# Decoder layer on one core: order of the negated pieces of u and of their adding transfers in the up projection

## The chip, the cores and the metric

The kernel runs on one core of one Trainium2 chip. The metric is the device time of one launch in microseconds (us), the median of several runs. Below, PE is TensorE (matmuls; PEld its weight loads), DVE is VectorE, ACT is ScalarE, POOL is GpSimd and SP is SyncE. SP, ACT and POOL each issue DMA transfers from their own instruction streams; a transfer that has to wait holds everything that stands behind it in that stream.

## The reference, cut to what matters

One decoder layer for 256 tokens of width 2048. Attention, the first residual and its norms come first; the change lies in the MLP behind them, with `d_ff` = 8192:

```
h = _rmsnorm(x, norm_mlp_pre[layer])
u = jnp.square(jax.nn.relu(h @ w_up[layer]))
x = x + _rmsnorm(u @ w_down[layer], norm_mlp_post[layer])
```

All data are float32. The kernel computes each product of float32 matrices from two rounded parts of each operand, hi = round(a) and lo = a - hi, as three matmuls: hi*hi, hi*lo, lo*hi.

## The kernel before

**Up projection.** The loop over `j` takes eight chunks of 1024 columns of `w_up`. A chunk accumulates four outputs of 128 tokens x 512 columns in PSUM (`acc_u`, for two token blocks b and two column halves n). Some 128-row blocks of the weights are multiplied directly ("k" steps, 12 matmuls each). Pairs of others go through a scheme with seven products instead of eight (`seven_products`, the "w" steps), for which DVE first builds sums of the weight blocks (`t` and `u` tiles, L361, L365, L366), and some of the products go to four more banks `m`. At a chunk's end `close` (L1052, L1055) combines the `m` banks into a tile `c`, and four DVE additions (L1121) put them into `acc_u`.

**Weights.** A "k" step's weights are loaded by SP into one of five `raw` buffers (512 KB). A "w" step's weights are loaded by POOL into one of two buffers, `ab` and `ab2` (1 MB, L374), or, in the last two chunks, partly by SP. ACT writes the hi part (L306, or L310 with a gain), and DVE the lo part (L307, L311). There are eight hi and eight lo buffers.

**Hand-over between chunks.** `up_evac` takes each `acc_u` of the finished chunk while PE already works on the next chunk: ACT writes r = relu(acc_u * scale) (L937) into one of two buffers `r`, PE transposes r (`rt`, L300), and ACT squares the transposes into the tile `uT` (L949; for some blocks the tile is called `u`, `ab` or `ab2`). The two halves n of chunk j give the blocks g = 2j and g = 2j+1 of u, each 128 x 1024.

**The low parts of u.** The down projection needs hi and lo of u. For every block g but the first, `lo_away(g)` prepares lo ahead of time in DRAM (`ukeep`): for each half h of the block, ACT writes -round(u) into an `r` buffer (`neg`, L960), ACT issues the write of it to `ukeep` (256 KB, L962), and POOL issues a transfer that adds u itself to the same place of `ukeep` (L964), so that u - round(u) stands there. POOL must wait for the write to land before it issues the add. Much later `split_u` brings the result back with one transfer per block (`ulo`, L976). `ukeep` transfers share POOL's stream with the loads of `ab` and `ab2`, and `neg` shares the two `r` buffers with `up_evac`.

**What sets the order.** There is no scheduler on the chip: each engine executes its instructions in the order in which the program wrote them. `Flow` sets that order while the program is built. The matmuls advance a planned clock (`flow.spend`); side work is written as generators whose `yield` gives the planned delay until their next piece; `pump` writes the pieces that have come due between two groups of matmuls. So a number in a `yield`, or the delay given to `flow.start`, decides behind which instructions a piece stands in its engine's stream, not when it runs.

Of the kernel before, what the change touches and what calls it, by code (L numbers as in the profile page):

```python
# [263 lines left out]
def layer(nc, tc, io):  # L264
    flow = Flow()
# [12 lines left out]
    def bank(i, name):  # L278
        return ps.tile([P, 512], F32, tag=f"bank{i}", bufs=1, name=name)
# [19 lines left out]
    def transpose(out, a):  # L299
        nc.tensor.transpose(out, a, ident)  # L300
        flow.spend(TR)
# [631 lines left out]
    def up_evac(j, b, i, acc, order):  # L933

        yield UP_STEP * order
        r = late["up"].tile([P, 512], F32, tag="r", bufs=2, name=f"r{j}_{b}")
        nc.scalar.activation(r, acc, AF.Relu, scale=rstd2[b])  # L937
        yield D_UP if j > 1 else 2 * D_UP
        t = bank(i, f"rt{j}_{b}")
        for k in range(4):  # L940
            transpose(t[:, k * P:(k + 1) * P], r[:, k * P:(k + 1) * P])
        if j not in uT:
            if j in (0, 1, 10, 11, 12, 13):
                t2 = late["u01" if j < 2 else "ab2" if j < 12 else "ab"][:, j % 2 * CW:(j % 2 + 1) * CW]
            else:
                tag = {"tag": "T", "bufs": 2} if j > 13 else {}
                t2 = late["up"].tile([P, CW], F32, name=f"uT{j}", **tag)
            uT[j] = t2.rearrange("p (k s) -> p k s", k=4)
        nc.scalar.activation(uT[j][:, :, b * P:(b + 1) * P], t.rearrange("p (k s) -> p k s", k=4), AF.Square)  # L949
        if b and j:  # L950
            flow.start(lo_away(j), 5.0 + 7.0 * (j % 2))

    def lo_away(g):

        ukeep[g] = dram.tile([P, CW], F32, name=f"ukeep{g}")
        u = uT[g].rearrange("p k s -> p (k s)")
        for h in range(2):
            c = slice(h * 512, (h + 1) * 512)
            t = late["up"].tile([P, 512], F32, tag="r", bufs=2, name=f"neg{g}_{h}")
            nc.scalar.activation(t.bitcast(F32R), u[:, c], AF.Copy, scale=-1.0)  # L960
            yield 1.0
            nc.scalar.dma_start(out=ukeep[g][:, c], in_=t)  # L962
            yield 9.0
            nc.gpsimd.dma_start(out=ukeep[g][:, c], in_=u[:, c], accum_op=OP.add)  # L964
            yield 2.0

# [96 lines left out]
    for j in range(FF // CW):  # L1063
# [9 lines left out]
        for t, b in order:  # L1073
# [19 lines left out]
            if what == "k":  # L1093
                w = weights.get(tiles[0])
                h_done(k, b)
                for n in range(2):
                    c = slice(n * 512, (n + 1) * 512)
                    three(accs[b, n], [tok(hT[x], k, b) for x in range(2)], [w[x][:, 0, c] for x in range(2)], t == 0, t == len(steps) - 1)
                    if j == 0 and t == len(steps) - 1:
                        evac.append(flow.start(up_evac(n, b, at[b, n], accs[b, n], 2 * b + n - 0.25 * (2 * b + n))))  # L1100
                    flow.pump()
                if b == NB - 1:
                    weights.free(tiles[0])
                continue
# [13 lines left out]
        if j:  # L1118

            for bn in PARTS:  # L1120
                nc.vector.tensor_tensor(out=accs[bn], in0=accs[bn], in1=more[bn], op=OP.add)  # L1121
            for o, (b, n) in enumerate(PARTS):
                evac.append(flow.start(up_evac(2 * j + n, b, at[b, n], accs[b, n], o + 0.6)))
# [194 lines left out]
```

## Time and profile before

| | |
|---|---|
| median of 3 runs | 1054.12 us (1051.59 to 1059.64) |
| profiled execution: its own time | 1057.15 us |
| profiled execution: span of the trace | 1055.2 us |
| granted TensorE clock, mean | 0.997 |
| busy in the span | PE 1035.3, DVE 834.4, ACT 645.3, POOL 90.0 us |
| up projection in the trace | roughly 365 to 715 us |
| down projection in the trace | roughly 715 to 1040 us |

Times in the trace count from the start of the span. A timeline row gives the start, the duration, the engine, the line and operation with output and input, how often, and in brackets the idle time of that engine just before and what ended it. A row of the chain of waits gives start, duration and what the end of the program was waiting for in that stretch.

### The profile page before, as it was taken

The numbers are of one execution on the slowest core, as the hardware profiler recorded it, in microseconds if no ns is written. First come the engines' busy times: TensorE is split into PE (matmuls) and PEld (weight loads), VectorE is DVE, ScalarE is ACT, GpSimd is POOL, SyncE is SP. The second block draws the span as 40 slices with busy tenths as digits, with TensorE's granted clock in tenths as the row PEclk, the third lists the DMA queues.
The fourth block names the chain that finished last, engine by engine and source line by source line (L and its number), as shares of the span: only waits on it lengthen the run. The fifth ranks groups of instructions, "written<-read, shape, count | busy, mean of one in ns | idle before, by whom it ended". The sixth has DMA issues, their size and how long they took to land.

```text
span 1055.2 us, 13457 instructions
## 1 busy us (share of the span) xinstructions
PE 1035.3 (98%) x4828; PEld 859.5 (81%) x4828; DVE 834.4 (79%) x1122; ACT 645.3 (61%) x884; POOL 90.0 (9%) x134
## 2 busy tenths in 40 slices
PE   9999999999999999999999999899999999999996
PEld 6888899888888788888877778787888888888885
DVE  6776546577556679998989889788889888998895
ACT  6675436566454567576756667667666664867661
POOL 0000000000000000111110111011110101111100
PEclk9999999999999999999999999999999999999998
DMA  9974546454356295758778687589997977789872
GB/s 303 369 232 147 147 131 222 145 175 152 129 197 221 86 374 160 242 169 287 221 235 251 201 249 196 189 273 353 305 333 271 358 251 244 287 302 344 339 240 80
DMA packets 89395, 248.21 MB, mean 235 GB/s; under 512 B 7920, under 2 KB 12528, under 8 KB 88944
## 3 DMA queue, kind: packets, MB, share of 16 engines
q1 hardware_dynamic: 61984, 162.03, 45.3%
q0 software_dynamic: 22592, 77.08, 23.4%
q10 hardware_dynamic: 4752, 8.24, 2.1%
q8 instruction: 38, 0.62, 0.2%
q14 instruction: 29, 0.24, 0.1%
HBM read 222.16 MB, written 25.17 MB: 234 GB/s over the span
## 4 chain that ended last, share of the span: by engine, by line
PE 78%; DVE 10%; DMA 6%; issue 3%; ACT 2%; POOL 0%; ACTq 0%; DVEq 0%; SPq 0%; POOLq 0%
PE y L296 24%; PE acc_u L296 11%; PE acc_o L296 8%; PE md L296 6%; PE acc_qk L296 4%; PE acc_v L296 4%; DVE lo L307 3%; PE m L296 3%; PE acc_ckv L296 2%; DVE lo L311 2%; DMA raw<-in_w_up 2%; PE acc_ukv L296 2%; PE acc_q L296 2%; PE acc_cq L296 2%; PE acc_k L296 2%
## 5 line engine op out<-in xcount | busy, mean ns | idle before, releaser
L307 DVE TENSOR_TENSOR lo<-raw,hi 128x1024 fp32r<-128x1024 f32 (+3 forms) x207 | 233.8, 1150 | 81.8 <-ACT hi L306 80.7
L306 ACT ACTIVATE hi<-raw 128x1024 fp32r<-128x1024 f32 (+3 forms) x207 | 203.4, 997 | 69.3 <-DMA raw<-in_w_in 14.4
L296 PE MATMUL acc_u<-hi,hT_hi 128*128 128x512 f32 x356 | 142.0, 399 | 0.4 <-DVE c L1055 0.4
L296 PE MATMUL acc_u<-hi,hT_lo 128*128 128x512 f32 x356 | 139.2, 391 | 0.4 <-DVE hT_lo L307 0.4
L296 PE MATMUL acc_u<-lo,hT_hi 128*128 128x512 f32 x356 | 138.8, 390 | 0.0
L296 PE MATMUL y<-hi,uhi 128*128 128x512 f32 x352 | 137.3, 390 | 0.0
L296 PE MATMUL y<-hi,ulo 128*128 128x512 f32 x352 | 137.0, 389 | 0.0
L296 PE MATMUL y<-lo,uhi 128*128 128x512 f32 x352 | 136.9, 389 | 0.0
L311 DVE SCALAR_TENSOR_TENSOR lo<-raw,gcol,hi 128x1024 fp32r<-128x1024 f32 x74 | 92.6, 1279 | 12.7 <-ACT hi L310 12.7
L310 ACT ACTIVATE hi<-raw,gcol 128x1024 fp32r<-128x1024 f32 x74 | 82.9, 1145 | 27.8 <-DMA raw<-in_w_up 21.1
L296 PEld LDWEIGHTS acc_u<-hi,hT_lo 128*128 128x128 f32 x356 | 66.8, 188 | 15.2 <-DVE hT_lo L307 0.8
L296 PEld LDWEIGHTS acc_u<-hi,hT_hi 128*128 128x128 f32 x356 | 66.9, 188 | 14.1 <-DVE c L1055 1.4
L296 PEld LDWEIGHTS acc_u<-lo,hT_hi 128*128 128x128 f32 x356 | 67.0, 188 | 12.7
L296 PEld LDWEIGHTS y<-lo,uhi 128*128 128x128 f32 x352 | 66.1, 188 | 13.7
L296 PEld LDWEIGHTS y<-hi,ulo 128*128 128x128 f32 x352 | 66.1, 188 | 13.7
L296 PEld LDWEIGHTS y<-hi,uhi 128*128 128x128 f32 x352 | 66.1, 188 | 13.6
L306 ACT ACTIVATE hi<-u 128x1024 fp32r<-128x1024 f32 (+1 forms) x38 | 37.6, 991 | 61.1 <-DVE u L366 47.4
L307 DVE TENSOR_TENSOR lo<-st_down,hi 128x1024 fp32r<-128x1024 f32 x48 | 57.6, 1220 | 1.5 <-ACT hi L306 1.5
L306 ACT ACTIVATE hi<-st_down 128x1024 fp32r<-128x1024 f32 x48 | 50.0, 1050 | 3.5 <-DVE st_down L366 1.1
L296 PE MATMUL md<-hi,s 128*128 128x512 f32 x144 | 52.1, 389 | 0.0
L296 PE MATMUL acc_o<-hi,mixT_hi 128*128 128x512 f32 x128 | 51.8, 405 | 0.0
L296 PE MATMUL acc_o<-hi,mixT_lo 128*128 128x512 f32 x128 | 50.2, 392 | 0.0
(330 smaller groups left out, 2167.9 us busy)
## 6 DMA issues: line engine op xcount, KB each, us to landing
raw<-in_w_down SPq DMA_DIRECT2D x80, 512.0 KB, 6.4
raw<-in_w_up SPq DMA_DIRECT2D x76, 512.0 KB, 5.8
raw<-in_w_in SPq DMA_DIRECT2D x55, 512.0 KB, 4.9
ab<-in_w_up POOLq DMA_DIRECT2D x22, 1024.0 KB, 8.0
raw<-in_w_out SPq DMA_DIRECT2D x32, 512.0 KB, 4.4
ulo<-ukeep POOLq DMA_DIRECT2D x30, 512.0 KB, 6.2
ab_down<-in_w_down POOLq DMA_DIRECT2D x13, 1024.0 KB, 9.4
ukeep<-neg ACTq DMA_DIRECT2D x30, 256.0 KB, 5.5
```

Source lines behind the costliest of these rows:

```text
L296: nc.tensor.matmul(out, a, b, start=start, stop=stop)
L306: nc.scalar.activation(hi, src, AF.Copy)
L307: nc.vector.tensor_tensor(out=lo, in0=src, in1=hi.bitcast(F32), op=OP.subtract)
L310: nc.scalar.activation(hi, src, AF.Copy, scale=g)
L311: nc.vector.scalar_tensor_tensor(out=lo, in0=src, scalar=g, in1=hi.bitcast(F32), op0=OP.mult, op1=OP.subtract)
```

## The change

In `up_evac`, `lo_away(j)` starts 2.0 planned us (even blocks) or 6.0 (odd blocks) after a block is complete, instead of 5.0 or 12.0. In `lo_away`, both halves are now negated and written first, with 8.0 planned us from one half to the next instead of 12.0, and only after a further 16.0 planned us are the two adding transfers issued, 2.0 apart.

```
@@ -948,7 +948,7 @@
         if b and j:
-            flow.start(lo_away(j), 5.0 + 7.0 * (j % 2))
+            flow.start(lo_away(j), 2.0 + 4.0 * (j % 2))
@@ -960,7 +960,10 @@
             nc.scalar.activation(t.bitcast(F32R), u[:, c], AF.Copy, scale=-1.0)
             yield 1.0
             nc.scalar.dma_start(out=ukeep[g][:, c], in_=t)
-            yield 9.0
+            yield 7.0
+        yield 16.0
+        for h in range(2):
+            c = slice(h * 512, (h + 1) * 512)
             nc.gpsimd.dma_start(out=ukeep[g][:, c], in_=u[:, c], accum_op=OP.add)
             yield 2.0
```

No instruction is added or removed. The streams of PE, DVE and SP keep their order; only ACT's and POOL's change. Behind the change, line numbers from L964 on are three higher. Three places follow.

POOL in chunk 3, from the load of its fourth pair of weight blocks (`ab2_3503`) to the load of chunk 4's third pair (`ab_3502`). `ukeep4` and `ukeep5` are the blocks that chunk 2 produced. Before:

```order
L374 DMA ab2_3503<-in_w_up 128x2x1024
L964 DMA ukeep4_4589<-uT4_4485 128x512
L964 DMA ukeep5_4672<-uT5_4505 128x512
L374 DMA ab_3502<-in_w_up 128x2x1024
L964 DMA ukeep4_4589<-uT4_4485 128x512
L964 DMA ukeep5_4672<-uT5_4505 128x512
L374 DMA ab2_3503<-in_w_up 128x2x1024
L374 DMA ab_3502<-in_w_up 128x2x1024
```

After:

```order
L374 DMA ab2_3503<-in_w_up 128x2x1024
L374 DMA ab_3502<-in_w_up 128x2x1024
L967 DMA ukeep4_4553<-uT4_4483 128x512 x2
L374 DMA ab2_3503<-in_w_up 128x2x1024
L967 DMA ukeep5_4621<-uT5_4503 128x512 x2
L374 DMA ab_3502<-in_w_up 128x2x1024
```

The load of chunk 4's first pair (`ab`, the second load shown) no longer has an add ahead of it, and the load of its second pair (`ab2`, the third load shown) stands behind the two adds of block 4 instead of behind all four.

ACT in chunk 3, from the last square of block 5 on. `hi192` to `hi195` are the hi parts of chunk 3's second pair, `hi197` and `hi198` those of its third. Before:

```order
L949 ACTIVATE uT5_4505<-rt5_1_4545 128x4x128
L306 ACTIVATE hi192_4558<-ab2_3503 128x512
L306 ACTIVATE hi193_4562<-ab2_3503 128x1024
L306 ACTIVATE hi194_4569<-u3_1_4520 128x1024
L306 ACTIVATE hi195_4579<-t3_1_4519 128x1024
L960 ACTIVATE neg4_0_4590<-uT4_4485 128x512
L310 ACTIVATE hi196_4600<-raw196_4598,gcol_69 128x1024
L962 DMA ukeep4_4589<-neg4_0_4590 128x512
L306 ACTIVATE hi197_4611<-ab_3502 128x512
```

After:

```order
L949 ACTIVATE uT5_4503<-rt5_1_4544 128x4x128
L960 ACTIVATE neg4_0_4554<-uT4_4483 128x512
L306 ACTIVATE hi192_4560<-ab2_3503 128x512
L306 ACTIVATE hi193_4564<-ab2_3503 128x1024
L306 ACTIVATE hi194_4572<-u3_1_4518 128x1024
L962 DMA ukeep4_4553<-neg4_0_4554 128x512
L306 ACTIVATE hi195_4583<-t3_1_4517 128x1024
L310 ACTIVATE hi196_4601<-raw196_4599,gcol_69 128x1024
L306 ACTIVATE hi197_4611<-ab_3502 128x512
L960 ACTIVATE neg5_0_4622<-uT5_4503 128x512
L962 DMA ukeep5_4621<-neg5_0_4622 128x512
```

The first half of block 4 is negated ahead of the second pair's hi parts instead of behind them, and its write is issued two rows earlier; the first half of block 5 moves forward from behind the third pair. The four halves of a chunk now end about where the third of them stood before. In chunk 7 the first `neg12` stands in the same way ahead of `uhi0`, the hi part of u's block 0.

ACT at the end of chunk 7, where `c_3504<-m1_7` opens the combination of the `m` banks (L1052 before, L1055 after). Before:

```order
L306 ACTIVATE hi302_6297<-raw302_6295 128x1024
L306 ACTIVATE hi303_6310<-raw303_6308 128x1024
L1052 ACTIVATE c_3504<-m1_7_6120 128x512
L306 ACTIVATE hi304_6327<-raw304_6325 128x1024
L960 ACTIVATE neg13_1_6334<-ab_3502 128x512
L962 DMA ukeep13_6212<-neg13_1_6334 128x512
L306 ACTIVATE hi305_6349<-raw305_6347 128x1024
```

After:

```order
L306 ACTIVATE hi302_6299<-raw302_6297 128x1024
L306 ACTIVATE hi303_6311<-raw303_6309 128x1024
L1055 ACTIVATE c_3504<-m1_7_6124 128x512
L306 ACTIVATE hi304_6328<-raw304_6326 128x1024
L306 ACTIVATE hi305_6346<-raw305_6344 128x1024
L306 ACTIVATE hi306_6380<-raw306_6378 128x1024
```

The last `neg` of the chunk and its write are gone from here; they stand eight rows ahead of `c<-m`. In chunks 2 to 6 the last `neg` stood directly ahead of `c<-m`, and has moved up likewise.

More of the change, by code (lines that the diff above doesn't have):

```diff
@@ L950, in up_evac @@
         if b and j:
-            flow.start(lo_away(j), 5.0 + 7.0 * (j % 2))
+            flow.start(lo_away(j), 2.0 + 4.0 * (j % 2))
     def lo_away(g):
@@ L962, in lo_away @@
             nc.scalar.dma_start(out=ukeep[g][:, c], in_=t)
-            yield 9.0
+            yield 7.0
+        yield 16.0
+        for h in range(2):
+            c = slice(h * 512, (h + 1) * 512)
             nc.gpsimd.dma_start(out=ukeep[g][:, c], in_=u[:, c], accum_op=OP.add)
```

## The prediction

> **What bounds the kernel now.** The page's first part comes first, because it says how much is to be had at all.
>
> ```profile
> PE 1035.3 (98%) x4828; PEld 859.5 (81%) x4828; DVE 834.4 (79%) x1122; ACT 645.3 (61%) x884; POOL 90.0 (9%) x134
> ```
>
> PE is busy for 1035.3 of 1055.2 us. The change leaves PE's work alone, so it can only touch the 19.9 us in which PE idles. PE's timeline, read next for its idle times, shows where the up projection has them:
>
> ```profile
> 538.48 0.66 PE L300 MATMUL rt<-ident,r 128*128 128x128 f32 x4 [1.25 <-ACT r L937]
> 576.72 0.51 PE L296 MATMUL acc_u<-hi,hT_hi 128*128 128x512 f32 x1 [0.43 <-DVE c L1055]
> 584.02 0.66 PE L300 MATMUL rt<-ident,r 128*128 128x128 f32 x4 [1.77 <-ACT r L937]
> 628.93 0.66 PE L300 MATMUL rt<-ident,r 128*128 128x128 f32 x4 [1.76 <-ACT r L937]
> 670.77 0.66 PE L300 MATMUL rt<-ident,r 128*128 128x128 f32 x4 [1.41 <-ACT r L937]
> 677.43 0.66 PE L300 MATMUL rt<-ident,r 128*128 128x128 f32 x4 [1.40 <-ACT r L937]
> 720.08 0.66 PE L300 MATMUL rt<-ident,r 128*128 128x128 f32 x4 [1.57 <-ACT r L937]
> ```
>
> All are hand-overs: chunks 3 to 4 (1.25), 4 to 5 (0.43 + 1.77), 5 to 6 (1.76), 6 to 7 (1.41 + 1.40), 7 to the down projection (1.57). Together 9.59 us, the most that this change can win there. Each waits for r, which waits for DVE's last additions into acc_u: DVE comes late to the chunk's end. Why, the chain of waits tells:
>
> ```profile
> 482.55 6.92 DMA ukeep<-neg
> ...
> 489.99 0.54 POOL ukeep L964
> 490.53 8.26 DMA ab<-in_w_up
> 498.88 1.24 DVE t L361
> ```
>
> The write of a negated piece takes 6.92 us; POOL stands before its add all that time; the load of the chunk's second pair stands behind the add, and DVE waits for the load. One chunk later the engines' timelines show the same:
>
> ```profile
> 534.67 0.87 POOL L964 DMA_DIRECT2D ukeep<-uT  x1 [7.47 <-DMA ukeep<-neg]
> 535.21 1.07 POOL L374 DMA_DIRECT2D ab<-in_w_up  x1
> 543.70 1.23 DVE L361 TENSOR_TENSOR t<-ab 128x1024 f32<-128x1024 f32 x1 [2.58 <-DMA ab<-in_w_up]
> ```
>
> **Part 1, the late loads.** In the new order the second pair's load stands behind the two adds of the even block only. The buffer it fills was last read in the second and third of these splits, and free at 518.26 + 1.82 = 520.1; the even block's second piece now stands right behind the first of them:
>
> ```profile
> 509.45 1.06 ACT L306 ACTIVATE hi<-u 128x1024 fp32r<-128x1024 f32 x1 [2.75 <-DVE u L366]
> 513.45 1.04 ACT L306 ACTIVATE hi<-ab 128x1024 fp32r<-128x1024 f32 x1
> 518.26 1.82 DVE L307 TENSOR_TENSOR lo<-ab,hi 128x512 fp32r<-128x512 f32 x2
> ```
>
> Its write so leaves ACT near 511 to 512, and with the 6.92 us above it has landed before the buffer is free. The load starts near 520 instead of 535.21 and lands 15 us earlier. DVE's wait at the chunk's front goes. What is late next is ACT: its hi parts of that pair follow the fourth square `uT<-rt`, which PE's transposes release. How far DVE is behind that square is seen in chunks 2 (no late load) to 6, square first, then DVE's split of u:
>
> ```profile
> 456.63 0.60 ACT L949 ACTIVATE uT<-rt 128x512 f32<-128x512 f32 x1 [1.03 <-PE rt L300]
> 459.87 1.22 DVE L307 TENSOR_TENSOR lo<-u,hi 128x1024 fp32r<-128x1024 f32 x1
> 499.33 0.60 ACT L949 ACTIVATE uT<-rt 128x512 f32<-128x512 f32 x1 [0.83 <-PE rt L300]
> 504.41 1.22 DVE L307 TENSOR_TENSOR lo<-u,hi 128x1024 fp32r<-128x1024 f32 x1
> 543.53 0.60 ACT L949 ACTIVATE uT<-rt 128x512 f32<-128x512 f32 x1 [0.50 <-PE rt L300]
> 549.23 1.22 DVE L307 TENSOR_TENSOR lo<-u,hi 128x1024 fp32r<-128x1024 f32 x1
> 589.07 0.60 ACT L949 ACTIVATE uT<-rt 128x512 f32<-128x512 f32 x1 [0.50 <-PE rt L300]
> 594.86 1.22 DVE L307 TENSOR_TENSOR lo<-u,hi 128x1024 fp32r<-128x1024 f32 x1
> 633.99 0.60 ACT L949 ACTIVATE ab<-rt 128x512 f32<-128x512 f32 x1 [0.51 <-PE rt L300]
> 639.36 1.22 DVE L307 TENSOR_TENSOR lo<-u,hi 128x1024 fp32r<-128x1024 f32 x1
> ```
>
> The distance is 3.24 us in chunk 2, and 5.08, 5.70, 5.79 and 5.37 in chunks 3 to 6: DVE could be 1.84, 2.46, 2.55 and 2.13 us earlier. But the first negated piece now stands between the square and the hi parts, and costs its duration there:
>
> ```profile
> L960 ACT ACTIVATE neg<-uT x20: 612/615/618, 460.5 to 751.3; 128x512 fp32r<-128x512 f32 x20
> ```
>
> With 0.6 off, DVE gains 1.2, 1.9, 1.9 and 1.5 us. Left of the stalls: 3 to 4, 1.25 - 1.2 = 0.05; 4 to 5, 2.20 - 1.9 = 0.3; 5 to 6 none; 6 to 7 the first (1.41) none, while the second comes 1.41 us sooner on PE and its r 1.5 us sooner, so 1.40 + 1.41 - 1.5 = 1.3.
>
> **Part 2, the end of chunk 7.** No `ab` load is late there. At its front the moved piece pushes the first of these rows back by 0.6, and at its end the second row goes, which is 0.6 again on the chain to r:
>
> ```profile
> 680.44 1.05 ACT L306 ACTIVATE uhi<-u 128x1024 fp32r<-128x1024 f32 x1
> 709.91 0.62 ACT L960 ACTIVATE neg<-ab 128x512 fp32r<-128x512 f32 x1
> ```
>
> I set it even, between 1.0 (only the end counts) and 2.2 (only the front): 1.57 stays. So 0.05 + 0.3 + 0 + 1.3 + 1.57 = 3.2 us remain, and the gain would be 9.6 - 3.2 = **6.4 us**, if nothing else moved.
>
> **Part 3, the crowd at the chunk's end.** The second pair's load (1 MB) and the adds now run at about 517 to 528 of chunk 3's time, where SP fetches the last `raw` blocks that DVE splits before the additions. These leave almost no slack:
>
> ```profile
> 517.06 1.28 DVE L311 SCALAR_TENSOR_TENSOR lo<-raw,gcol,hi 128x1024 fp32r<-128x1024 f32 x1
> 522.27 6.07 DVE L311 SCALAR_TENSOR_TENSOR lo<-raw,gcol,hi 128x1024 fp32r<-128x1024 f32 x5
> 524.92 1.15 ACT L310 ACTIVATE hi<-raw,gcol 128x1024 fp32r<-128x1024 f32 x1 [0.99 <-DMA raw<-in_w_up]
> 563.18 7.79 DMA raw<-in_w_up
> 572.26 1.28 DVE L311 SCALAR_TENSOR_TENSOR lo<-raw,gcol,hi 128x1024 fp32r<-128x1024 f32 x1 [0.31 <-ACT hi L310]
> 668.10 1.28 DVE L311 SCALAR_TENSOR_TENSOR lo<-raw,gcol,hi 128x1024 fp32r<-128x1024 f32 x1 [2.21 <-ACT hi L310]
> ```
>
> The first row frees the buffer for the last fetch of chunk 3, at 518.3, and ACT uses it at 524.92: 6.6 us. In chunk 3 ACT ends the last of the five at 526.07, and DVE takes it about 1.0 later, the slack. In chunk 4 the fetch took 7.79 and DVE waited 0.31; in chunk 6 it waited 2.21. If the fetch takes x us longer, chunks 4 and 6 pay x, chunks 3 and 5 pay x - 1.0 (chunk 5, which shows no such wait, taken as chunk 3). The price was not measured in the new order. The nearest row is the landing of `raw` between 500 and 700 us, min, median, max; the second is over the whole run:
>
> ```profile
> DMA to landing us min/median/max: 3.4/6.2/9.2
> DMA to landing us min/median/max: 2.7/5.1/13.3
> ```
>
> From 7.79, x lies between -1.2 (the 6.6 us of chunk 3's fetch) and +1.4 (the 9.2). In the other direction the first pair's load leaves this stretch, by 5 us, so the bytes nearly balance; what is added are adds. I take x = +1.0, nearer the upper end because DVE is then waiting on the last of several. That costs 1.0 + 1.0 = 2.0 us, which leaves **4.4 us** of gain. The ends give 2.9 (x = 1.4) and 7.9 (x = -1.2).
>
> The Trainium skill (DMA: Bandwidth & Descriptors, section Queues, rings and completion order) says that a DMA engine serves the queues that have work in turn, packet by packet. By that, more transfers behind each other in POOL's queue would not slow SP's. By it the sum is 6.4. The two fetches above, of 6.6 and 7.8 us, each ran beside one 1 MB load and do not decide it.
>
> **Costed at nothing.** The odd block's second piece waits, as before, for an `r` buffer, that is for its first write to land:
>
> ```profile
> DMA to landing us min/median/max: 2.0/5.5/8.3
> ```
>
> By the order the two stand some 7 us apart (an estimate); at 8.3 ACT is held for 1.3 us. Behind it stands the hi of `ab` that ran at 513.45, which DVE wants near 519.1: 4 us of cover, and beyond that each us is paid on DVE. The adds that now come later are wanted only by the `ulo` transfers of the down projection, and the writes have landed before POOL reaches them.
>
> **Rivals.** *No crowd*: x = 0, 1054.12 - 6.4 = **1047.7**; for it, the moved first load frees the stretch; against it, the waits of 0.31 and 2.21 are already those of full traffic. *All stalls go*, 9.6: **1044.5**; for it, DVE's work in a chunk is less than PE's once nothing is late; against it, the hand-overs after chunks 6 and 7 have fetches and an ACT queue of their own. *The wait only changes place*: at x = 2 the rests are 1.05, 2.3, 0.9, 3.3 and 1.57, 9.1 together, the gain 0.5, **1053.6**; for it, 2.21 us of DVE's wait in chunk 6 are of this kind; against it, 9.8 us is more than any fetch here took. The same result comes if the adds still block the load, should the even writes land 9 us late. *Slower*: the same fetch at the run's longest, 13.3 (x = 5.5); chunks 3 to 6 then pay 20 us more, less the 6.4: about 13.5 lost, **1067.6**. It turns at x = 2.1, a fetch of 9.9 us; against it, 13.3 came once, and not here.
>
> **How the numbers follow.** The sums are against the profiled execution's own 1057.15 us, which makes 1052.8; it lies 3.0 above the median of the runs, 1054.12, and from that I predict 1054.12 - 4.4 = **1049.7**. Chances: forecast 0.48, no crowd 0.17, all stalls go 0.12, wait changes place 0.18, slower 0.05. The range takes in all but the last, with about 1 to 3 us for the spread of runs (1051.59 to 1059.64 before): **1043.5 to 1056.5**. A measurement of this kernel tells about 1% from no change, 10.5 us. More than that cannot come from 9.6 us, only from all of them with luck in the runs: 0.06. Slower by over 1%: 0.05. Within: 0.89.
>
> **What will show it.** Right: POOL starts a chunk's second `ab` load some 15 us earlier; no DVE wait for `ab` at the fronts of chunks 3 to 6; the distance from square to split of u near 3.8; PE's stall after chunk 3 gone and those after 4 and 5 below 1.3. DVE waits on the last `raw` fetch of chunks 4 and 6 grow by about 1 us. Wrong: the stalls stay while the wait moves to `raw` (crowd under-costed), or vanish also after chunks 6 and 7 (crowd over-costed), or ACT's hi parts wait on `neg`.

## The result and the profile after

The changed kernel takes **1050.07 us**, the median of 14 runs (1048.38 to 1051.71); 14 runs of the kernel before give 1057.32 us (1051.59 to 1061.42). The ratio is **0.9934, with a 95% interval of 0.992 to 0.9948**: 7.0 us less (5.5 to 8.5). The profiled execution took 1049.74 us, against 1057.15 before: 7.41 less. Two later sessions gave 0.9939 (0.9921 to 0.9956) and 0.9933 (0.9915 to 0.9952).

First the totals of the page. PE's work is the same; the span around it is 1047.9 us instead of 1055.2.

```profile
PE 1035.3 (99%) x4828; PEld 860.3 (82%) x4828; DVE 834.0 (80%) x1122; ACT 644.5 (62%) x884; POOL 90.4 (9%) x134
```

Then PE's timeline, all rows with idle time from 480 us on. Of seven stalls before (9.59 us) one is left. Two waits are new, in the down projection.

```profile
669.53 0.66 PE L300 MATMUL rt<-ident,r 128*128 128x128 f32 x4 [0.65 <-ACT r L937]
894.04 0.50 PE L296 MATMUL y<-lo,uhi 128*128 128x512 f32 x1 [0.74 <-DVE lo L307]
976.98 0.50 PE L296 MATMUL y<-hi,ulo 128*128 128x512 f32 x1 [0.80 <-DMA ulo<-ukeep]
```

8.94 us went and 1.54 came: 7.40, next to the 7.41 between the two executions. That holds for this one profile. In the two later profiles of the changed kernel the stall after chunk 6 is 1.38 and 1.30, the one from chunk 7 to the down projection is not gone but 0.72 and 0.27 (1.57 before), and the two waits in the down projection are absent once and 0.25 and 0.75 the other time. The cause is seen on POOL, in chunk 3: the load of the second pair starts at 519.60, not 535.21, and waits only for its buffer (DVE's lo), not for a write.

```profile
519.60 0.74 POOL L374 DMA_DIRECT2D ab<-in_w_up  x1 [3.39 <-DVE lo L307]
520.33 0.91 POOL L967 DMA_DIRECT2D ukeep<-uT  x1
524.35 0.85 POOL L967 DMA_DIRECT2D ukeep<-uT  x1 [3.12 <-DMA ukeep<-neg]
```

At the front of chunk 4 DVE then finds the load there. What it waits for is ACT, in two places of 0.28 and 0.26 us; between ACT's square and the hi parts stands the moved `neg`. (The second wait comes with only the adds moved too, 0.25 there; the first, of 0.28, does not.)

```profile
542.74 0.60 ACT L949 ACTIVATE uT<-rt 128x512 f32<-128x512 f32 x1 [0.49 <-PE rt L300]
543.23 0.63 ACT L960 ACTIVATE neg<-uT 128x512 fp32r<-128x512 f32 x1
544.40 0.69 DVE L307 TENSOR_TENSOR lo<-ab,hi 128x512 fp32r<-128x512 f32 x1 [0.28 <-ACT hi L306]
545.35 1.23 DVE L307 TENSOR_TENSOR lo<-ab,hi 128x1024 fp32r<-128x1024 f32 x1 [0.26 <-ACT hi L306]
546.50 1.22 DVE L307 TENSOR_TENSOR lo<-u,hi 128x1024 fp32r<-128x1024 f32 x1
```

The ends of the chunks: the five splits of `raw` in chunks 3 and 4 run without a gap, and in chunk 6 the wait is 1.45 (2.21 before). In chunk 6 ACT waits 4.70 for the last `raw` fetch (5.71 before), in chunk 7 4.84 (6.53 before). DVE waits 7.89 for `ab_down` at 719 (3.62 before), and PE loses nothing to it.

```profile
521.49 6.06 DVE L311 SCALAR_TENSOR_TENSOR lo<-raw,gcol,hi 128x1024 fp32r<-128x1024 f32 x5
564.35 6.06 DVE L311 SCALAR_TENSOR_TENSOR lo<-raw,gcol,hi 128x1024 fp32r<-128x1024 f32 x5
659.02 1.16 ACT L310 ACTIVATE hi<-raw,gcol 128x1024 fp32r<-128x1024 f32 x1 [4.70 <-DMA raw<-in_w_up]
660.21 1.28 DVE L311 SCALAR_TENSOR_TENSOR lo<-raw,gcol,hi 128x1024 fp32r<-128x1024 f32 x1 [1.45 <-ACT hi L310]
685.38 1.15 ACT L310 ACTIVATE hi<-raw,gcol 128x1024 fp32r<-128x1024 f32 x1 [4.84 <-DMA raw<-in_w_up]
719.04 1.22 DVE L361 TENSOR_TENSOR st_down<-ab_down 128x1024 f32<-128x1024 f32 x1 [7.89 <-DMA ab_down<-in_w_down]
```

### The profile page after: what moved, and what is told of

The parts are those of the page before. It is cut to its first block, busy times and chain, and to the rows that moved or that the text cites. A ratio compares the mean times of both kernels' runs of the same rounds, so it can differ in the third digit from the quotient of the medians.

```text
span 1047.9 us, 13455 instructions
## 1 busy us (share of the span) xinstructions
PE 1035.3 (99%) x4828; PEld 860.3 (82%) x4828; DVE 834.0 (80%) x1122; ACT 644.5 (62%) x884; POOL 90.4 (9%) x134
## 4 chain that ended last, share of the span: by engine, by line
PE 86%; DVE 6%; DMA 3%; issue 2%; ACT 2%; SPq 0%; POOL 0%; DVEq 0%; POOLq 0%; ACTq 0%
PE acc_u L296 21%; PE y L296 20%; PE acc_o L296 8%; PE m L296 6%; PE md L296 5%; PE acc_v L296 4%; PE acc_qk L296 4%; DVE lo L307 3%; PE acc_ckv L296 2%; PE acc_ukv L296 2%; PE acc_q L296 2%; PE acc_cq L296 2%; PE acc_k L296 2%; PE acc_uq L296 2%; PE rt L300 1%
## 5 line engine op out<-in xcount | busy, mean ns | idle before, releaser
L311 DVE SCALAR_TENSOR_TENSOR lo<-raw,gcol,hi 128x1024 fp32r<-128x1024 f32 x74 | 92.4, 1278 | 11.1 <-ACT hi L310 11.0
```

Of the source, the lines that this page charges most:

```text
L311: nc.vector.scalar_tensor_tensor(out=lo, in0=src, scalar=g, in1=hi.bitcast(F32), op0=OP.mult, op1=OP.subtract)
```

## The experiments

The theory is the held load: DVE is late because one load stands on POOL behind adds that wait for writes. The rivals: ACT's order alone makes the gain, or the number of transfers in one place does. The runs were made in three sessions, each on one chip beside the kernel before, which took 1058.22, 1056.63 and 1056.58 us there; so times of different sessions can be set side by side only to within some 1.6 us.

| run | median, us | ratio to before (95%) |
|---|---|---|
| only the adds moved, first session | 1047.71 | 0.990 (0.987 to 0.9929) |
| only the negated pieces moved | 1051.80 | 0.9942 (0.9919 to 0.9965) |
| before, no adds | 1046.95 | 0.9897 (0.9867 to 0.9927) |
| after, no adds | 1049.36 | 0.9913 (0.988 to 0.9946) |
| changed kernel, second session | 1049.84 | 0.9939 (0.9921 to 0.9956) |
| one add ahead of the load | 1053.74 | 0.9963 (0.9949 to 0.9977) |
| chunk 7's adds early | 1050.95 | 0.9945 (0.9926 to 0.9964) |
| delays 5.0 and 9.0 | 1048.72 | 0.9926 (0.9908 to 0.9944) |
| only the adds moved, third session | 1047.81 | 0.9908 (0.9891 to 0.9925) |
| delays 5.0 and 9.0, third session | 1048.40 | 0.9913 (0.9895 to 0.9931) |
| changed kernel, third session | 1050.82 | 0.9933 (0.9915 to 0.9952) |
| doubled crowd | 1052.57 | 0.9956 (0.9935 to 0.9976) |

### Each half of the change alone

Only the adds moved: against the kernel before, the pieces keep their places and the adds take those of the changed kernel.

```
             nc.scalar.dma_start(out=ukeep[g][:, c], in_=t)
-            yield 9.0
+            yield 11.0
+        yield 5.0 - 3.0 * (g % 2)
+        for h in range(2):
+            c = slice(h * 512, (h + 1) * 512)
             nc.gpsimd.dma_start(out=ukeep[g][:, c], in_=u[:, c], accum_op=OP.add)
```

> The negated pieces and their writes stand on ACT where they stood before; only the adds stand later on POOL, where the change puts them. Held load (my theory: DVE is late because the second ab2 load of a chunk stands on POOL behind adds that wait for the writes of negated pieces): the load now stands behind the two adds of the even block alone, whose second write leaves ACT at 518.9 in chunk 3 and lands 5 to 8 us later, so the load starts at 524 to 527 instead of 535.2. Before, DVE waited 2.58 us for it, so every start ahead of 532.6 ends that wait: 6 to 8 us less than the kernel before, as with the whole change. ACT's order (rival: the gain comes from the last negated piece, which no longer stands ahead of c<-m at the chunk's end): that piece still stands there, so no gain, 0 to 1 us.

Only the pieces moved: against the changed kernel, the adds go back to the planned times of before.

```
-            yield 7.0
-        yield 16.0
+            yield 7.0 * (1 - h)
+        yield 4.0 + 3.0 * (g % 2)
         for h in range(2):
             c = slice(h * 512, (h + 1) * 512)
             nc.gpsimd.dma_start(out=ukeep[g][:, c], in_=u[:, c], accum_op=OP.add)
-            yield 2.0
+            yield 12.0
```

> The negated pieces and their writes stand on ACT where the change puts them; the adds keep the planned times of before, so that the ab2 load stands behind all four of them again. Held load: the last of the four writes leaves ACT at 516.5 of chunk 3 instead of 526.6 and lands 4 to 9 us later, so the load starts at 521 to 526, still ahead of 532.6: 6 to 8 us less than before. ACT's order: the same 6 to 8 us, since its order is that of the change. A third reading, that it is the place of the adds on POOL alone which counts: 0 to 2 us. With the run that only moves the adds, the three readings give (gain, gain), (none, gain) and (gain, none).

Both gain, 10.5 and 6.4 us by the medians, which is (gain, gain): the held load. POOL's timeline in chunk 3, first with only the adds moved, then with only the pieces moved, has the load within 1 us of the expected stretches (524 to 527 and 521 to 526), both ahead of 532.6:

```profile
522.62 0.88 POOL L967 DMA_DIRECT2D ukeep<-uT  x1 [9.34 <-DMA ukeep<-neg]
523.20 1.05 POOL L374 DMA_DIRECT2D ab<-in_w_up  x1
```

```profile
525.58 0.86 POOL L967 DMA_DIRECT2D ukeep<-uT  x1 [8.62 <-DMA ukeep<-neg]
526.12 1.05 POOL L374 DMA_DIRECT2D ab<-in_w_up  x1
```

POOL still waits 9.34 and 8.62 us, but early enough. What had not been expected: the half that moves only the adds gains more than the 6 to 8 us, and is faster than the whole change. PE's timeline of it has one stall left in these chunks, that of the other half three:

```profile
669.18 0.66 PE L300 MATMUL rt<-ident,r 128*128 128x128 f32 x4 [0.50 <-ACT r L937]
```

```profile
538.30 0.66 PE L300 MATMUL rt<-ident,r 128*128 128x128 f32 x4 [0.46 <-ACT r L937]
670.61 0.66 PE L300 MATMUL rt<-ident,r 128*128 128x128 f32 x4 [1.11 <-ACT r L937]
713.22 0.66 PE L300 MATMUL rt<-ident,r 128*128 128x128 f32 x4 [1.50 <-ACT r L937]
```

### No adds at all

In both kernels the one line with `accum_op=OP.add` was taken out, so that u is never added to -round(u).

> The kernel before, with the adding transfers left out (so the low parts of u are not u - round(u) but -round(u)); negated pieces and writes stay where they were. Held load: POOL has nothing to wait for, the load starts when its buffer is free, near 520, DVE's waits for ab at the fronts of chunks 3 to 6 are gone: 6 to 8 us less than before, the same as with the adds moved, within 1 us. ACT's order: 0 to 1 us. If the adds also cost by their traffic, this run gains over 1 us more than the one that only moves them.

> The changed kernel with the adding transfers left out (low parts of u are -round(u)). Crowd (the term of the forecast, 2.0 us: the adds lengthen the last raw fetches at the end of chunks 3 to 6): 2 us or more less than the changed kernel, so about 9 less than before, and ACT's wait for raw in chunk 6 (4.70) and DVE's behind it (1.45) get shorter by about 1. No crowd: within 1 us of the changed kernel, about 7 less than before, those waits as they are, except that the new wait of PE for ulo in the down projection (0.80) may come or go.

Before without adds: 1046.95, 0.8 us from the kernel that only moves them (1047.71) in the same session. So nearly all that could be had from POOL's waits is had by moving the adds. After without adds: 1049.36, against 1050.07, 1049.84 and 1050.82 with them (in other sessions): 0.5 to 1.5 less, not 2. In the time the crowd of the forecast is not there. In the profile the sign that was named for it is: at the end of chunk 6 ACT waits 0.71 us for the last `raw` fetch, not 4.70, and DVE's 1.45 behind it and PE's stall 6 to 7 are gone.

```profile
655.42 1.15 ACT L310 ACTIVATE hi<-raw,gcol 128x1024 fp32r<-128x1024 f32 x1 [0.71 <-DMA raw<-in_w_up]
```

That fetch lands 3.6 us after its issue here, and 5.3 in the kernel before without adds, where PE's stall is gone too. With adds it takes 7.6, 8.5 and 8.2 in the three profiles of the changed kernel, 7.9 with only the adds moved, and 8.3 before the change. So the adds do lengthen it, and with them comes PE's stall 6 to 7, 0.40 to 1.38 us in the profiles of the kernels whose adds are all late. But adds ran beside that fetch before the change as well: the crowd is real at the end of chunk 6, and it did not grow. PE's wait for `ulo` near 977 comes in both kernels without adds (0.9 and 1.0 us), so it is not the adds' lateness that makes it.

### One of four adds put back ahead of the load

```
-            yield 9.0
+            yield 11.0 - 2.0 * (g % 2) * h
+        yield 5.0 * (1 - g % 2)
+        for h in ((1, 0) if g % 2 else (0, 1)):
+            c = slice(h * 512, (h + 1) * 512)
             nc.gpsimd.dma_start(out=ukeep[g][:, c], in_=u[:, c], accum_op=OP.add)
-            yield 2.0
+            yield 2.0 + 2.0 * (g % 2)
```

Against the kernel before, the odd block's second half is added at its planned time of before; the other three adds stay late.

> As the run that only moved the adds, with one of a chunk's four adds put back ahead of the ab2 load: the one that waits for the last write (ACT 526.6 in chunk 3). Held load: POOL stands before it until that write has landed, the load starts near 535 as before, DVE waits 2 to 2.7 us again at the fronts of chunks 3 to 6, and the stalls 3 to 4, 4 to 5, 5 to 6, 6 to 7 (8.0 us before) are back: 7 to 9 us slower than with all adds moved, 1 to 3 us below before. If it is the number of transfers crowded before the load that counts, one of four gives back a quarter: about 2.5 us slower than with all moved.

5.9 us slower than with all adds moved (1053.74 against 1047.8 in the other two sessions), short of the expected 7 to 9, and more than twice the quarter's 2.5; 2.9 below the kernel before in the same session. The load of chunk 3 started just at the edge, that of chunk 4 past it; DVE's wait and PE's stalls answer to that: DVE waits for `ab` at the fronts of chunks 3, 5 and 6 (1.74, 2.53 and 2.58 us) and not of chunk 4, and PE stalls after chunks 3, 5 and 6 and not after chunk 4.

```profile
531.48 1.76 POOL L967 DMA_DIRECT2D ukeep<-uT  x2 [17.32 <-DMA ukeep<-neg]
532.59 1.39 POOL L374 DMA_DIRECT2D ab<-in_w_up  x1
...
577.30 1.39 POOL L374 DMA_DIRECT2D ab<-in_w_up  x1
...
585.94 1.22 DVE L361 TENSOR_TENSOR t<-ab 128x1024 f32<-128x1024 f32 x1 [2.53 <-DMA ab<-in_w_up]
```

```profile
538.40 0.66 PE L300 MATMUL rt<-ident,r 128*128 128x128 f32 x4 [0.71 <-ACT r L937]
625.54 0.66 PE L300 MATMUL rt<-ident,r 128*128 128x128 f32 x4 [1.48 <-ACT r L937]
666.76 0.66 PE L300 MATMUL rt<-ident,r 128*128 128x128 f32 x4 [0.80 <-ACT r L937]
673.42 0.66 PE L300 MATMUL rt<-ident,r 128*128 128x128 f32 x4 [1.38 <-ACT r L937]
```

Over the kernels (whose times at chunk 3's front differ by under 1 us), starts of 519.6, 523.2, 526.1 and 532.6 cost DVE no wait at chunk 4's front, 535.2 cost 2.58: a load may be held for 13 us for nothing, and beyond that DVE waits. One transfer held is enough, since it holds the stream.

### Chunk 7

As with only the adds moved, but for blocks from 12 on each add stands behind its write as before:

```
             yield 9.0
+            if g >= 12:
+                nc.gpsimd.dma_start(out=ukeep[g][:, c], in_=u[:, c], accum_op=OP.add)
+            yield 2.0
+        if g >= 12:
+            return
+        yield 5.0 - 3.0 * (g % 2)
...
```

> As the run that only moved the adds, with the adds of the blocks that are written in chunk 7 (and later) back at their old times; no load of chunk 7 stands behind them. Crowd in chunk 7: one add then runs beside the raw fetch that ACT waits for near 685 to 694; the fetch takes 6.7 us as before instead of 4.7 (ACT's wait 6.5 instead of 4.6), DVE's additions come 1 to 2 us later, and PE's wait for r at the hand-over from chunk 7 to the down projection, 1.57 before and absent with the adds moved, is back at 0.8 to 1.6: 1 to 1.6 us slower than with all moved. Inherited lateness (the 1.57 came from chunk 6 and before): no such wait, the same time within 0.5 us.

The mechanism came as forecast: the fetch that SP issued at 679.22 reached ACT at 685.76 (6.54 us; 679.47 to 684.21, 4.74, with the adds moved), and the hand-over to the down projection stalls again. ACT's row and PE's:

```profile
685.76 1.15 ACT L310 ACTIVATE hi<-raw,gcol 128x1024 fp32r<-128x1024 f32 x1 [6.38 <-PE m L296]
```

```profile
711.28 0.66 PE L300 MATMUL rt<-ident,r 128*128 128x128 f32 x4 [1.24 <-ACT r L937]
```

(The wait is put down to PE here, which had long been done.) The DMA view of 678 to 688 us shows why: queue 0, which is POOL's, has one add of 0.26 MB in it. First this kernel, then the one with the adds moved, whose queue 0 is empty; the last column of the issues is the median landing in us.

```profile
q1 hardware_dynamic: 573, 2.09, 64.8%
q0 software_dynamic: 144, 0.26, 17.8%
...
raw<-in_w_up SPq DMA_DIRECT2D x3, 512.0 KB, 7.8
```

```profile
q1 hardware_dynamic: 576, 2.10, 63.4%
q10 hardware_dynamic: 135, 0.25, 6.8%
...
raw<-in_w_up SPq DMA_DIRECT2D x3, 512.0 KB, 5.4
```

The time missed: 3.1 to 3.2 us slower (1050.95, against 1047.81 and 1047.71 in the other sessions), where 1 to 1.6 were expected. In its profile 2.1 us more are PE's waits for `lo` in the down projection. Waits of that kind, 0.3 to 1.7 us, came and went over the runs, in two profiles of the changed kernel and not in the third; whether the early adds of the last blocks lengthen them stays open.

### What the earlier pieces cost

The first piece back behind the hi parts, the last one still off the chunk's end, the adds as in the changed kernel:

```
-            flow.start(lo_away(j), 2.0 + 4.0 * (j % 2))
+            flow.start(lo_away(j), 5.0 + 4.0 * (j % 2))
...
-        yield 16.0
+        yield 13.0
```

> The changed kernel with the first pieces negated three planned us later (delays of 5.0 and 9.0 instead of 2.0 and 6.0, then 13.0 instead of 16.0, so that the adds keep the changed kernel's times). The first negated piece then stands behind the second pair's hi parts, not ahead of them, and the last one still well ahead of c<-m. If the piece ahead of the hi parts is what the changed kernel loses against the run that only moved the adds (0.6 us of ACT at each chunk's front): 1.5 to 3 us less than the changed kernel, the same as with only the adds moved within 0.7 us. If the closer spacing is what costs (writes bunched together): as the changed kernel, 6 to 8 us less than before.

> The changed kernel once more, so that it and the three below are timed on one chip beside the same runs of before. Expected: 6 to 8 us less than before, and 2 to 3 us more than the run that only moved the adds (1047.71) gave. Its profile should again show the DVE rows of a chunk's second pair 0.25 to 0.3 us behind ACT in two places, and PE losing under 0.2 us in each chunk to them. If PE's new waits in the down projection (0.74 for lo, 0.80 for ulo, at 894 and 977 us in the first profile) belong to the change, they come again at the same places; if they are chance, they do not.

> The run that only moved the adds once more, beside the changed kernel and the one with delays of 5.0 and 9.0, on one chip. If the first negated piece ahead of the hi parts is what the changed kernel loses: 1.5 to 2.5 us less than the changed kernel, and like the 5.0 and 9.0 kernel within 1 us. If the first measurement was a matter of the chip: within 1 us of the changed kernel.

> The kernel with delays of 5.0, 9.0 and 13.0 once more. The first piece is behind the hi parts as in the kernel before, the last one is off the chunk's end as in the changed kernel; if each is worth its 0.6 us on the chain, it is the fastest of the three, 0 to 1 us below the one that only moved the adds and 1 to 2.5 below the changed kernel.

> The changed kernel, for the same comparison: 1049.5 to 1050.5, 6 to 8 us below before.

In the second session 1048.72 against 1049.84, a gain of 1.1 where 1.5 to 3 was expected; in the third 1047.81 (adds only), 1048.40 (5.0 and 9.0) and 1050.82 (changed kernel): 3.0 (1.5 to 2.5 was expected) and 2.4 less than the change, which itself was 5.8 below the kernel before there, not 6 to 8. The piece ahead of the hi parts does cost. The two kernels without adds say the same in one session: 1049.36 with the pieces in their new places, 1046.95 with them in the old ones, 2.4 apart with no add in either. That the 5.0 and 9.0 kernel would be the fastest of the three was not borne out; its runs and those of the adds alone overlap (1046.89 to 1049.38, 1047.36 to 1048.11). The cost is seen where PE's list of idle times shows nothing, in DVE's period. The same row of chunks 4 and 5 in the changed kernel, and then with only the adds moved:

```profile
545.35 1.23 DVE L307 TENSOR_TENSOR lo<-ab,hi 128x1024 fp32r<-128x1024 f32 x1 [0.26 <-ACT hi L306]
588.22 1.23 DVE L307 TENSOR_TENSOR lo<-ab,hi 128x1024 fp32r<-128x1024 f32 x1 [0.26 <-ACT hi L306]
```

```profile
544.99 1.23 DVE L307 TENSOR_TENSOR lo<-ab,hi 128x1024 fp32r<-128x1024 f32 x1 [0.25 <-ACT hi L306]
587.69 1.22 DVE L307 TENSOR_TENSOR lo<-ab,hi 128x1024 fp32r<-128x1024 f32 x1 [0.26 <-ACT hi L306]
```

42.87 us a chunk against 42.70. It is 42.70 also with 5.0 and 9.0 and 42.69 in the kernel before without adds, but 42.88 with only the pieces moved and in the changed kernel without adds: the period goes with the place of the first piece, not with the adds. Over chunks 3 to 6 that is 0.7 us. The stall 6 to 7 was 0.65, 1.38 and 1.30 in three profiles of the changed kernel, 0.50 and 0.61 with only the adds moved: 0.55 more. The one from chunk 7 to the down projection (0, 0.72 and 0.27 against none) makes 0.3. Waits in the down projection (1.54, 0 and 1.00 against 0 and 0.44) make 0.6. These 2.2 us are most of the 2 to 3. Only the 0.7 comes alike in every profile; what makes the rest change from profile to profile stays open.

### The crowd doubled

Only the adds moved, and behind every add of blocks 1 to 13 one more transfer:

```
+            if g < 14:
+                more = dram.tile([P, 512], F32, name=f"more{g}_{h}")
+                nc.gpsimd.dma_start(out=more, in_=io["w_up"][h * P:(h + 1) * P, g * 512:(g + 1) * 512])
```

> The kernel that only moved the adds, with one more transfer of 256 KB behind every add of the blocks 1 to 13 (a copy of a piece of w_up from DRAM to DRAM that nobody reads), so 1 MB more for each chunk in the place of the crowd. Crowd as the forecast had it (four adds lengthen the last raw fetch by 1.0 us, DVE has at most 1.0 us to spare): 1 to 2 us or more slower than without, longer waits of ACT for raw at the ends of chunks 4 and 6. Served in turn, so that a longer POOL queue does not slow SP's: within 0.5 us, the raw waits as they are.

4.8 us slower (1052.57 against 1047.81). That is a loss, far beyond the 0.5 us that was expected of queues served in turn; but it does not lie where the crowd would have it. DVE's wait at the end of chunk 6 is the 1.76 us of the kernel without the copies; at the fronts DVE waits once for `ab`, 0.83 us. PE's stalls are in the down projection, behind `ulo`:

```profile
659.64 1.28 DVE L311 SCALAR_TENSOR_TENSOR lo<-raw,gcol,hi 128x1024 fp32r<-128x1024 f32 x1 [1.76 <-ACT hi L310]
```

```profile
729.89 0.50 PE L296 MATMUL y<-hi,ulo 128*128 128x512 f32 x1 [2.96 <-DMA ulo<-ukeep]
980.50 0.50 PE L296 MATMUL y<-hi,ulo 128*128 128x512 f32 x1 [1.41 <-DMA ulo<-ukeep]
```

At 703 to 715 us the copies and the last adds stand on POOL ahead of `ulo`, which there goes out at 714.98 instead of about 708. So more transfers behind each other on POOL did not slow the fetch that DVE splits last: in chunks 3, 4 and 6 it landed in 4.7, 4.0 and 7.9 us (4.0, 4.1 and 7.9 without the copies). The fetches issued after it did land later, two of chunk 6 in 12.6 and 13.6 us instead of 11.0 and 11.1; PE's one stall there was 0.84 us (0.50 and 0.61 without). The cover of the late adds ends where `ulo` begins.

## Why the prediction was right, and where it was not

**What bounds the kernel, and the mechanism**: right. PE's idle time in the hand-overs (9.59 us) was the prize, the held load the cause of most of it; taken away in three ways (adds moved, pieces moved, adds left out) it gave 6.4 to 11.3 us by the medians, and put back with one add it took 5.9.

**Part 1, the late loads**: right in kind. The load went from 535.21 to 519.60 (forecast: 15 us earlier), no DVE wait for `ab` was left, the distance from square to split of u is 546.50 - 542.74 = 3.76 (forecast 3.8). The stalls 3 to 4, 4 to 5 and 5 to 6 are gone (rest forecast 0.35, and 0.17 us a chunk stand outside the list). For 6 to 7, 1.3 was forecast and 0.65 to 1.38 came.

**Part 2, chunk 7 set even**: wrong by 0.85 to 1.57. Of the 1.57 left standing, 0, 0.72 and 0.27 came in the three profiles. Its front did lose 0.5 (`ulo` waits 1.89 for `uhi` instead of 1.37), but the term left out the adds that leave chunk 7's fetches: 6.7 us from issue to use before, 5.05 after. Putting them back brought 1.24 of the stall back. So in chunk 7 the crowd worked the other way round, as a gain.

```profile
674.15 1.23 DVE L307 TENSOR_TENSOR ulo<-u,uhi 128x1024 fp32r<-128x1024 f32 x1 [1.89 <-ACT uhi L306]
```

**Part 3, x = +1.0**: the step that failed. The last fetches did not take 1.0 us longer. They landed in 7.1 and 6.9 us in chunks 3 and 4 (6.4 and 7.8 before), and in 7.6, 8.5 and 8.2 in the three profiles of chunk 6 (8.3 before). DVE's wait behind them was 1.45 us in chunk 6 of this profile (2.38 and 2.07 in the other two, 2.21 before), and none in chunks 3 to 5. So x lay between -0.9 and +0.7, about 0, the 2.0 us were not there, and the sum of 6.4 lies inside the interval of 5.5 to 8.5; the forecast 4.4 does not. The premise that failed is that the adds are new beside these fetches. They do lengthen the one of chunk 6, which took 3.6 us without any, but the kernel before too issued an add within 2.5 us of each of them (POOL at 517.20, 560.73 and 658.53, SP at 518.37, 563.18 and 658.47). In chunk 6, where DVE waits for it, the cost was already in the time before.

The Trainium skill (DMA: Bandwidth & Descriptors, section Queues, rings and completion order) has each DMA engine take the queues with work in turn. By it a longer POOL queue does not slow an SP fetch that lands while that queue still has work, and an add in a POOL queue that was empty takes a share from it; the runs fit both (landings of 7.9 and 7.9 us with and without the copies in chunk 6, of 5.4 and 7.8 in chunk 7).

**The base.** 1049.7 lies near 1050.07 by luck, through two misses that offset each other: the gain was 2.6 us larger than forecast, and the median of three runs from which it was taken, 1054.12, lay 3.2 below that of 14.

**Costed at nothing**: the wait of a piece for an `r` buffer never held ACT's hi parts in front of DVE; right. The later adds found their cover; the doubled crowd showed its end. New is what the sum did not have: 1.54 us of waits in the down projection. They changed from profile to profile and came without adds too.

**The rivals.** No crowd (1047.7) had the right sum, though the crowd is there in both kernels and only its growth is not. All stalls go (1044.5) comes close to the kernel that only moves the adds, which kept 0.50 us of them. That the wait changes place, or grows past the gain, did not happen.

## What to carry to other kernels

A transfer that waits holds everything behind it in its engine's stream, so look at what stands behind a waiting issue before looking at the transfer itself; move the waiting one behind the loads, to just ahead of its own reader. When a change has two halves, time each alone: here moving the adds was worth 8.8 to 10.5 us, and moving the pieces with them gave 2 to 3 back. A transfer that is found to cost something in the new order may have cost the same in the old one: look for it in both profiles before adding it to the sum. After the listed stalls are gone, compare the period of a loop on the next engine (42.87 against 42.70), which shows a loss that no idle time does.

## What the runs showed of the hardware that was not expected

In 10 us of chunk 7 one adding transfer of 0.26 MB took 17.8% of the 16 DMA engines' time; in the other kernel the write of 0.25 MB took 6.8%: 2.6 times as much for the same bytes counted, though the `raw` fetches ran beside the add and hardly beside the write. From 676 to 700 us of the kernel with chunk 7's adds early, two adds took 13.4% for 0.52 MB and three writes 9.4% for 0.79 MB, again about twice as much for each byte. Three `raw` fetches of 512 KB beside the one add landed in 7.8 us instead of 5.4.

The last fetch of chunk 6 landed in 3.6 and 5.3 us with no adds on POOL, in 7.6 to 8.5 with them, and in 7.9 with as many bytes of copies behind them: the adds on one queue cost a fetch on another 2.6 to 4.9 us (with the pieces in the same places), and twice the bytes did not cost it more.
